# Attention scores copied out of PSUM by ScalarE, and products of a constant at the kernel's start

## The chip, the core and the metric

The kernel runs on one core of a Trainium2 chip. Five engines work side by side, each in the order of its own instructions, and wait for each other by semaphores: TensorE (PE in the profile; its weight loads are listed as PEld), VectorE (DVE), ScalarE (ACT), GpSimd (POOL) and SyncE (SP, which here issues DMAs). Matmul results land in PSUM, eight banks of 2 KB in each partition; TensorE, VectorE and ScalarE work on them there, or on SBUF. The metric is the device time of one execution in microseconds, as the median of several runs. One more execution was profiled; its rows are what the sections below quote.

## The reference

One block of a hybrid decoder, 528 positions (16 learned tokens and 512 real ones) of width 2048. An input projection feeds a state-space mixer and an attention of 16 heads with 64 channels each; both are normalised and go through one output projection, and a gated MLP with a short convolution follows. The part that the change touches is the attention:

```python
z = jnp.einsum('bqhd,bkhd->bhqk', q_blk, k).astype(jnp.float32) * scale
valid = (kpos[None, :] < qpos[:, None])[None, None]
log_keep = jnp.where(valid, jax.nn.log_sigmoid(-z), 0.0)
suffix = lax.cumsum(log_keep, axis=3, reverse=True) - log_keep
w = jnp.where(valid, jnp.exp(jax.nn.log_sigmoid(z) + suffix), 0.0)
return jnp.einsum('bhqk,bkhd->bqhd', w.astype(v.dtype), v)
```

There is no softmax: a reversed running sum over the keys of log(1 + exp(z)) is subtracted from the score, and Exp of that is the weight.

## The kernel before

**Dense work and lanes.** Nearly all of the time is dense products: weights come as tiles of 128 x 1024 floats, are split into a high part (a cast on ScalarE, line 242, tile wh) and a low part (a subtraction on VectorE through the helper of line 117, tile wl), and each product is three matmuls (lines 320 to 322). The attention is no stage of its own. It is a Python generator, `att_lane`, that is stepped between dense products: `pulse` adds up the time of the products issued, and every 900 ns of it one step of the lane is written into the program. So the order of each engine's instructions is fixed when the kernel is built, and dense products stand between the pieces of attention.

**Units and items.** A unit is four heads, and there are four units, 0 to 3. `Unit.items` lists what is done for one: item (0, all four heads), two items of two heads for the second chunk of queries, four items of one head for the third and four for the fourth, and the item None for the last 16 queries. An item goes through four steps, each later by the steps in LAGS (2, 4, 6), while the next items start every two steps:

- `stage_a`: TensorE puts the mask into a bank with a product of a mask and an identity (line 958), then adds the scores (line 969). ScalarE computes Abs of them out of PSUM, then Exp and Ln in SBUF (tile at).
- `stage_a2`: VectorE adds max(z, 0), runs the scan (lines 996 and 999) and subtracts the sum from z (through line 117). Both the first and the last of these read z in PSUM.
- `stage_b`: TensorE transposes the result into a further bank (line 1026; line 1016 for item None), and ScalarE takes its Exp out of that bank.
- `stage_c`: TensorE multiplies with the values (line 1065), VectorE copies the result out (line 1072).

**Banks.** The pool psz has four banks (tag z). An item of the first two chunks takes two of them for its scores; of the third and fourth chunk every second item takes two, one of which (`self.second`) serves the item after it. The transposes take one. A bank is given to a new tile when the readers of the old one are done.

**Other work there.** During units 0 and 1 the dense products are the rest of the input projection, during units 2 and 3 the output projection; then GpSimd adds squares for the next norm (`acc_square`).

**The start.** SyncE issues the loads of x, of the vector tile vec and of the first weights. ScalarE needs x and vec for the first operand. GpSimd fills constants; steady, a tile of ones, is the first operand of the scans.

Of the kernel before, what the change touches and what calls it, by code (L numbers as in the profile page):

```python
# [15 lines left out]
AF = mybir.ActivationFunctionType  # L16
# [44 lines left out]
def build(tc, io, nslots=67, manual=True):  # L61
    nc = tc.nc
    ctx = ExitStack()
    with ctx:
# [51 lines left out]
        def sub(e, out, a, b):  # L116
            e.tensor_tensor(out, a, b, op=ALU.subtract)  # L117
# [16 lines left out]
        def make_consts():  # L134
            G.memset(steady, 1.0)
            S.copy(identb, ident)
# [729 lines left out]
        class Unit:  # L866


            def __init__(self, u):
                self.u = u  # L870
                self.ks, self.qs, self.vts = [], [], []
                self.st, self.yps = {}, {}

# [54 lines left out]
            def stage_a(self, it):  # L928

                if it is None:  # L930
                    n, m = 64, L
                    z = slot([P, L])[:64]
                    for x in range(2):
# [10 lines left out]
                        else:  # L944
                            S.copy(z[:, 264:512], b[:, :248])
                            add(V, z[:, 512:], b[:, 248:], mask5)
                    z = [z]
                else:
# [4 lines left out]
                    if hs[0] % 2 == 0:  # L953
# [8 lines left out]
                        for p in (0, 1) if j == 0 else (hs[0] // 2,):  # L962
                            (kh, kl), (qh, ql) = self.ks[p], self.qs[p]["Q"]
                            for i_, (qq, kk, o) in enumerate(
                                ((self.qf[p], self.kf[p], a),) if j == 0 else ((qh, kh, a - 13), (qh, kl, a - 13), (ql, kh, a - 13))
                            ):
                                for i in range(2):
# [4 lines left out]
                                    )  # L972
                        if j > 1:

                            self.second = zs.pop()
                    else:
                        zs = [self.second]
                    if j == 0:
                        self.kf = self.qf = None
                    z = [b.rearrange("p h k -> p (h k)") for b in zs]  # L980
                t = at_tile(n, m)
                w = m // len(z)
                for x, b in enumerate(z):
                    act(t[:, w * x : w * x + w], b, AF.Abs)
                act(t, t, AF.Exp, scale=-1.0)
# [3 lines left out]
            def stage_a2(self, it):  # L989

                z, t, n, m = self.st[it]
                c = at_tile(n, m)
                w = m // len(z)
                for x, b in enumerate(z):
                    r = slice(w * x, w * x + w)
                    V.scalar_tensor_tensor(t[:, r], b, 0.0, t[:, r], op0=ALU.max, op1=ALU.add)
                w = m if it is None else m // len(it[1])
                for x in range(0, m, w):
                    V.tensor_tensor_scan(
                        c[:, x : x + w][:, ::-1], steady[:n, :w], t[:, x : x + w][:, ::-1], 0.0, op0=ALU.mult, op1=ALU.add  # L1000
                    )
                w = m // len(z)
                for x, b in enumerate(z):
                    r = slice(w * x, w * x + w)
                    sub(V, c[:, r], b, c[:, r])
                self.st[it] = c
# [148 lines left out]
        def square_x(k):  # L1155
# [7 lines left out]
            xraw[k] = None  # L1163

        G.memset(epsc, EPS)
        act(cst.tile([P, 1], F32, name="warm"), epsc, AF.Square)

        load_x(0)
        nc.sync.dma_start(vec, io["vec"])
        fetch(0)  # L1170
        load_x(1)
# [531 lines left out]
```

## Time and profile before

| | us |
|---|---|
| median of 3 runs | 2230.75 (2229.09 to 2231.03) |
| profiled execution | 2228.46 |
| its span, first to last instruction | 2226.7 |
| TensorE busy | 2163.8 (97%) |
| VectorE busy | 1567.0 (70%) |
| ScalarE busy | 1032.5 (46%) |
| GpSimd busy | 209.6 (9%) |
| mean granted clock of TensorE, as a share of full speed | 0.991 |

Times in the rows below are microseconds from the start of the span unless ns is written. Busy time of TensorE is modelled at its ends and includes work at the lower clock, so it says less than it seems to. A row of the timeline gives start, duration, engine, line, operation, what is written and read, a count where equal instructions were merged, and in brackets how long the engine stood idle before it and which instruction ended that. In a table of waits the time is idle time of the waiting engine. A wait for several semaphores is put down to the one that came last.

### The profile page before, as it was taken

Reading aid. Unit: us, or ns where it says so; the run is one execution under the profiler, and the core shown is the slowest. Engines: PE = TensorE matmul, PEld = TensorE weight load, DVE = VectorE, ACT = ScalarE, POOL = GpSimd, SP = SyncE. Lnnn points to the kernel's source line nnn. Section 1 sums busy time; section 2 is a strip of 40 time slices with the busy share of each in tenths; the row PEclk is TensorE's granted clock in tenths of the full one; section 3 lists DMA queues with packets and bytes.
Section 4 is the critical chain, followed back from the end, with each engine's and each line's share of the span. In section 5 each row is a group of like instructions: output and inputs, shape, how many; then the busy total and the mean of one; then the engine's idle time right before and its main releaser. Section 6 shows DMA issues by size and latency. Waiting matters only on the chain.

```text
span 2226.7 us, 39757 instructions
## 1 busy us (share of the span) xinstructions
PE 2163.8 (97%) x16204; PEld 2049.5 (92%) x16204; DVE 1567.0 (70%) x2387; ACT 1032.5 (46%) x1648; POOL 209.6 (9%) x290
## 2 busy tenths in 40 slices
PE   8999999999889999999999999999999999999997
PEld 8999998889778999999999999999999888888887
DVE  7977785765668668788778877887788544444464
ACT  6255444655555455555555555555555222222235
POOL 0000000001112231111101110111010000000004
PEclk9999999999889999999999999999999999999999
DMA  6433333332323357777777777777777533333342
GB/s 220 123 111 101 116 101 120 101 120 96 101 67 119 129 166 180 194 194 207 185 194 200 200 187 193 196 203 188 194 197 206 183 121 118 119 113 120 116 142 76
DMA packets 118806, 335.10 MB, mean 150 GB/s; under 512 B 13024, under 2 KB 25696, under 8 KB 118624
## 3 DMA queue, kind: packets, MB, share of 16 engines
q1 hardware_dynamic: 100288, 269.56, 37.9%
q0 software_dynamic: 17472, 61.89, 13.6%
q8 instruction: 127, 2.08, 0.4%
q10 hardware_dynamic: 864, 1.11, 0.2%
q14 instruction: 55, 0.45, 0.1%
HBM read 300.23 MB, written 32.28 MB: 149 GB/s over the span
## 4 chain that ended last, share of the span: by engine, by line
PE 62%; DVE 2%; ACT 1%; issue 1%; DVEq 0%; ACTq 0%
PE d L321 15%; PE d L320 15%; PE d L322 15%; PE z L321 4%; PE z L320 4%; PE z L322 4%; PE y L321 2%; PE y L322 2%; PE y L320 2%; DVE s L117 0%; DVE wl L117 0%; ACT s L1359 0%; ACT wh L242 0%; ACT s L105 0%; DVE s L114 0%
## 5 line engine op out<-in xcount | busy, mean ns | idle before, releaser
L320 PE MATMUL d<-s,wh 128*128 128x258 f32 (+4 forms) x3456 | 1063.5, 308 | 12.1 <-ACT wh L242 5.6
L321 PE MATMUL d<-s,wh 128*128 128x258 f32 (+4 forms) x3456 | 1057.4, 306 | 1.2 <-DVE s L117 1.2
L322 PE MATMUL d<-s,wl 128*128 128x258 f32 (+4 forms) x3456 | 1052.7, 305 | 1.2 <-DVE wl L117 1.2
L320 PEld LDWEIGHTS d<-s,wh 128*128 128x128 f32 x3456 | 656.4, 190 | 43.8 <-ACT wh L242 7.8
L322 PEld LDWEIGHTS d<-s,wl 128*128 128x128 f32 x3456 | 660.2, 191 | 29.9 <-DVE wl L117 1.8
L321 PEld LDWEIGHTS d<-s,wh 128*128 128x128 f32 x3456 | 658.2, 190 | 30.9 <-DVE s L117 2.5
L242 ACT CAST wh<-wr 128x1024 fp32r<-128x1024 f32 (+2 forms) x209 | 197.4, 945 | 426.6 <-PE d L321 340.9
L117 DVE TENSOR_TENSOR wl<-wr,wh 128x1024 fp32r<-128x1024 f32 (+2 forms) x209 | 232.8, 1114 | 86.5 <-ACT wh L242 86.5
L114 DVE TENSOR_TENSOR s<-s,d 128x512 f32<-128x512 f32 (+2 forms) x176 | 103.6, 589 | 264.1 <-PE d L322 258.9
L321 PE MATMUL z<-s,wh 128*128 128x258 f32 (+1 forms) x768 | 219.5, 286 | 0.0
L320 PE MATMUL z<-s,wh 128*128 128x258 f32 (+1 forms) x768 | 218.7, 285 | 0.5 <-ACT s L1434 0.5
L322 PE MATMUL z<-s,wl 128*128 128x258 f32 (+1 forms) x768 | 217.7, 283 | 0.5 <-DVE wl L117 0.5
L117 DVE TENSOR_TENSOR wl<-wu,wh 128x1024 fp32r<-128x1024 f32 x132 | 161.4, 1223 | 2.8 <-ACT wh L242 2.7
L114 POOL TENSOR_TENSOR s<-s,s 128x514 f32<-128x514 f32 (+1 forms) x73 | 85.0, 1165 | 799.8 <-ACT s L105 669.7
L320 PE MATMUL y<-s,wh 128*128 128x258 f32 (+1 forms) x544 | 155.7, 286 | 0.0
L322 PE MATMUL y<-s,wl 128*128 128x258 f32 (+1 forms) x544 | 154.4, 284 | 1.2 <-DVE wl L117 1.2
L321 PE MATMUL y<-s,wh 128*128 128x258 f32 (+1 forms) x544 | 154.5, 284 | 0.0
L242 ACT CAST wh<-wu 128x1024 fp32r<-128x1024 f32 x132 | 138.8, 1052 | 32.6 <-ACT s L105 32.6
L322 PEld LDWEIGHTS z<-s,wl 128*128 128x128 f32 x768 | 146.6, 191 | 0.7 <-DVE wl L117 0.7
L321 PEld LDWEIGHTS z<-s,wh 128*128 128x128 f32 x768 | 146.9, 191 | 0.0
L320 PEld LDWEIGHTS z<-s,wh 128*128 128x128 f32 x768 | 145.1, 189 | 0.7 <-ACT s L1434 0.7
L117 DVE TENSOR_TENSOR wl<-wu_s,wh 128x1024 fp32r<-128x1024 f32 x88 | 107.5, 1222 | 41.8 <-ACT wh L242 41.8
(224 smaller groups left out, 2769.2 us busy)
## 6 DMA issues: line engine op xcount, KB each, us to landing
wu<-w_up SPq DMA_DIRECT2D x132, 512.0 KB, 5.3
wu_s<-w_up SPq DMA_DIRECT2D x88, 512.0 KB, 4.8
wu_s<-w_up POOLq DMA_DIRECT2D x88, 512.0 KB, 7.4
wr<-w_down SPq DMA_DIRECT2D x96, 384.0 KB, 3.0
wr<-w_in SPq DMA_DIRECT2D x63, 512.0 KB, 4.2
wr<-w_out SPq DMA_DIRECT2D x32, 512.0 KB, 3.9
fact<-s POOLq DMA_DIRECT2D x44, 256.0 KB, 3.1
s<-fact SPq DMA_DIRECT2D x44, 256.0 KB, 3.4
```

The source lines that it names most:

```text
L114: e.tensor_tensor(out, a, b, op=ALU.add)
L117: e.tensor_tensor(out, a, b, op=ALU.subtract)
L242: S.copy(hi[:, r], raw[:, r])
L320: PE.matmul(ps, whi, xhi, start=start, stop=False, **kw)
L321: PE.matmul(ps, whi, xlo, start=False, stop=False, **kw)
L322: PE.matmul(ps, wlo, xhi, start=False, stop=stop, **kw)
```

## The change

**In attention.** `stage_a` takes a slot in SBUF for each item (for two items where one pair of banks serves two), and ScalarE copies the banks there as soon as its turn comes. Abs, the addition of max(z, 0) and the last subtraction read that copy, each with one instruction for an item. The bank of the second item of a pair is copied together with the first one's, and the copy waits in the list `self.zs`.

**At the start.** The memset of steady moves from `make_consts` to the very beginning, ahead of that of epsc. The load of vec is issued by ScalarE ahead of its table load and no longer by SyncE between x and the weights. Nine FP32 products of steady with itself, 264 columns each, into a bank that nobody reads, stand first on TensorE.

```diff
         def make_consts():
-            G.memset(steady, 1.0)
             S.copy(identb, ident)
...
-                        if j > 1:
-
-                            self.second = zs.pop()
-                    else:
-                        zs = [self.second]
+
+                        z = None
+                        for x, b in enumerate(zs):
+                            if z is None or j > 1:
+                                z = slot([P, 528])[:n, :m]
+                                self.zs.append(z)
+                            S.copy(z[:, nh * k * x : nh * k * (x + 1)] if j < 2 else z, b.rearrange("p h k -> p (h k)"))
+                    z = self.zs.pop(0)
...
-                    z = [b.rearrange("p h k -> p (h k)") for b in zs]
                 t = at_tile(n, m)
-                w = m // len(z)
-                for x, b in enumerate(z):
-                    act(t[:, w * x : w * x + w], b, AF.Abs)
+                act(t, z, AF.Abs)
...
-                w = m // len(z)
-                for x, b in enumerate(z):
-                    r = slice(w * x, w * x + w)
-                    V.scalar_tensor_tensor(t[:, r], b, 0.0, t[:, r], op0=ALU.max, op1=ALU.add)
+                V.scalar_tensor_tensor(t, z, 0.0, t, op0=ALU.max, op1=ALU.add)
...
-                w = m // len(z)
-                for x, b in enumerate(z):
-                    r = slice(w * x, w * x + w)
-                    sub(V, c[:, r], b, c[:, r])
+                sub(V, c, z, c)
...
+        G.memset(steady, 1.0)
         G.memset(epsc, EPS)
+
+        nc.scalar.dma_start(vec, io["vec"])
+        load_x(0)
+        fetch(0)
         act(cst.tile([P, 1], F32, name="warm"), epsc, AF.Square)
 
-        load_x(0)
-        nc.sync.dma_start(vec, io["vec"])
-        fetch(0)
+        ps = bank([P, 264])
+        for i in range(9):
+            PE.matmul(ps, steady[:, :P], steady[:, :264], start=True, stop=True)
         load_x(1)
```

The order of TensorE's instructions is otherwise as it was. What changes there is who ends its waits. On TensorE, at the third item of unit 0 (masks into two banks of the pool z, scores, then the transposes of the first item, whose operand is the tile at; the bracket names the engines waited for), there stands before:

```order
L958 LDWEIGHTS identb [waits DVE_49]
L958 MATMUL z_4970<-mask,identb 128x128 [waits PE_49]
L958 LDWEIGHTS identb [waits DVE_49]
L958 MATMUL z_4971<-mask,identb 128x128 [waits PE_49]
...
L1026 MATMUL z_4985<-consts,at_4946 128x116 [waits DVE_49,PE_49]
```

and now:

```order
L956 LDWEIGHTS identb
L956 MATMUL z_4982<-mask,identb 128x128 [waits Activation_49]
L956 LDWEIGHTS identb
L956 MATMUL z_4983<-mask,identb 128x128 [waits Activation_49]
...
L1018 MATMUL z_4999<-consts,at_4960 128x116 [waits DVE_49,Activation_49]
```

The masks waited for VectorE and now wait for ScalarE (Activation); the transposes wait for VectorE and, for their bank, for ScalarE.

On ScalarE, at the first two items of unit 0 (s is a slot in SBUF, at the working tile), before:

```order
L105 ACTIVATE at_4907<-z_4899 116x256 [waits PE_49]
L105 ACTIVATE at_4907<-z_4900 116x256 [waits PE_49]
L101 ACT_TABLE_LOAD
L105 ACTIVATE at_4907<-at_4907 116x512 [waits Activation_49] x2
L105 ACTIVATE at_4941<-z_4931 128x256 [waits PE_49]
L105 ACTIVATE at_4941<-z_4932 128x256 [waits PE_49]
L105 ACTIVATE at_4941<-at_4941 128x512 [waits Activation_49] x2
```

and now:

```order
L977 COPY s_4917<-z_4909 116x256 [waits PE_49]
L977 COPY s_4917<-z_4910 116x256 [waits PE_49]
L105 ACTIVATE at_4920<-s_4917 116x512 [waits Activation_49]
L101 ACT_TABLE_LOAD
L105 ACTIVATE at_4920<-at_4920 116x512 [waits Activation_49] x2
L977 COPY s_4953<-z_4943 128x256 [waits PE_49]
L977 COPY s_4953<-z_4944 128x256 [waits PE_49]
L105 ACTIVATE at_4956<-s_4953 128x512 [waits Activation_49]
L105 ACTIVATE at_4956<-at_4956 128x512 [waits Activation_49] x2
```

Two copies stand ahead of each Abs, which is now one instruction.

## Rows read from the trace of the kernel before

**Rows 1.** The page, part 1: busy us, share of the span, instructions

```profile
PE 2163.8 (97%) x16204; PEld 2049.5 (92%) x16204; DVE 1567.0 (70%) x2387; ACT 1032.5 (46%) x1648; POOL 209.6 (9%) x290
```

**Rows 2.** Table of waits of TensorE: waited for, us in total, times, longest us

```profile
PE z L1026 <- DVE at L117: 25.5, 14, 4.2
PE z L958 <- DVE at L117: 4.7, 6, 1.6
PE z L1016 <- DVE at L117: 2.4, 2, 1.8
```

**Rows 3.** Timeline, unit 0: start us, us, engine, line, operation [idle before, releaser]

```profile
379.39 1.36 DVE L999 TENSOR_TENSOR_SCAN at<-steady,at 116x128 f32<-116x128 f32 x4
380.67 0.73 DVE L117 TENSOR_TENSOR at<-z,at 116x256 f32<-116x256 f32 x2
381.12 0.56 PE L958 MATMUL z<-mask,identb 128*128 128x128 bf16 x2 [0.63 <-DVE at L117]
383.16 0.72 DVE L117 TENSOR_TENSOR at<-z,at 128x256 f32<-128x256 f32 x2
383.70 0.49 PE L1026 MATMUL z<-consts,at 116*128 116x116 f32 x3 [1.46 <-DVE at L117]
...
390.61 0.66 PE L1026 MATMUL z<-consts,at 128*128 128x128 f32 x4 [2.72 <-DVE at L117]
```

**Rows 4.** Timeline, unit 2, where GpSimd adds squares

```profile
561.65 3.48 DVE L999 TENSOR_TENSOR_SCAN at<-steady,at 116x128 f32<-116x128 f32 x4
561.82 2.71 POOL L114 TENSOR_TENSOR s<-s,s 128x514 f32<-128x514 f32 x2 [9.32 <-ACT s L105]
565.50 0.56 PE L958 MATMUL z<-mask,identb 128*128 128x128 bf16 x2 [0.72 <-DVE at L117]
570.81 1.01 PE L1026 MATMUL z<-consts,at 116*128 116x116 f32 x4 [4.19 <-DVE at L117]
```

**Rows 5.** Busy time by stretch at half clock: length, engines (count), PEclk, DMA share, GB/s

```profile
443.80:447.10 3.30, 3.30 (x18) 3.11 (x16) 1.22 (x1) 1.15 (x2) 0.00 (x0) 0.50 0.00 0
...
652.00:655.30 3.30, 2.85 (x13) 2.85 (x14) 2.71 (x6) 1.63 (x4) 0.00 (x0) 0.50 0.00 0
sum 33.30, PE 30.04 PEld 28.64 DVE 15.37 ACT 9.10 POOL 2.40; mean PE 3.76 PEld 3.58 DVE 1.92 ACT 1.14 POOL 0.30
```

**Rows 6.** ScalarE's groups by shape, 350 to 860 us: count, busy us, mean ns, idle

```profile
L915 ACT COPY s<-z 128x512 f32<-128x512 f32 x8 | 4.7, 583 | 5.9 <-PE z L914 5.9
L1309 ACT COPY s<-d 128x256 f32<-128x256 f32 x2 | 0.7, 358 | 0.0
```

**Rows 7.** Busy time by stretch, as in rows 5: unit 0; units 2 and 3

```profile
374.30:433.70 59.40, 52.80 (x491) 46.79 (x490) 41.86 (x77) 37.70 (x74) 0.00 (x0) 1.00 0.25 82
...
552.00:693.50 141.50, 120.46 (x1047) 108.22 (x1045) 98.76 (x171) 78.87 (x155) 21.48 (x24) 0.90 0.28 93
```

**Rows 8.** VectorE's groups by shape, units 2 and 3, columns as in rows 6

```profile
L117 DVE TENSOR_TENSOR at<-z,at 128x512 f32<-128x512 f32 x8 | 5.5, 691 | 0.3
L117 DVE TENSOR_TENSOR at<-z,at 116x256 f32<-116x256 f32 x4 | 1.4, 399 | 0.0
L117 DVE TENSOR_TENSOR at<-s,at 64x528 f32<-64x528 f32 x2 | 1.4, 700 | 0.1
```

**Rows 9.** Timeline of the start, and two pairs of FP32 products at full clock

```profile
0.77 0.54 POOL L135 MEMSET steady<- 128x528 f32 x1
4.19 0.73 ACT L415 ACTIVATE s<-s,vec 128x528 fp32r<-128x528 f32 x1 [1.96 <-DMA vec<-vec]
5.64 0.59 PE L320 MATMUL d<-s,wh 128*128 128x264 f32 x1 [5.64 <-ACT wh L242]
...
10.33 0.29 PE L322 MATMUL d<-s,wl 128*128 128x264 f32 x1
...
41.04 0.61 PE L368 MATMUL y<-s,consts 128*128 128x264 f32 x2
41.49 0.61 PE L368 MATMUL z<-s,consts 128*128 128x264 f32 x2
```

More of the change, by code (lines that the diff above doesn't have):

```diff
@@ L871, in __init__ @@
                 self.ks, self.qs, self.vts = [], [], []
-                self.st, self.yps = {}, {}
+                self.st, self.yps, self.zs = {}, {}, []
             def load(self, what):
@@ L946, in stage_a @@
                             add(V, z[:, 512:], b[:, 248:], mask5)
-                    z = [z]
                 else:
```

## The prediction

> **What bounds the kernel now.** I read the page first, then the table of waits of TensorE, then stretches of the timeline, and last the groups by shape. TensorE is busy for 97% of the span and the chain that ended last is almost all TensorE [rows 1]; the reader should conclude that the only time to win is where TensorE stands idle or runs at its lower clock. The table of waits says where it stands: 25.5 us ahead of the transposes of L1026, 4.7 us ahead of the mask products of L958 and 2.4 us ahead of L1016, 32.6 us together, all put down to the subtraction of stage_a2 on VectorE [rows 2]. That is all in attention, between 374 and 693 us.
>
> The timeline of unit 0 tells what is waited for. The third item's mask product starts at 381.12, in the middle of the first item's pair of subtractions (380.67 to 381.40): it reads nothing that they write, it wants a bank of which they are the last readers. The transposes of the first item start at 383.70, though their operand was complete at 381.40; what ended just then is the first half of the *second* item's pair (383.16 to 383.88). The transposes of the second item start at 390.61 after 2.72 us [rows 3]. So at these places TensorE waits for a bank of the pool z, four banks of which two items hold two each from their scores to their subtraction. Unit 0 loses 0.63 + 0.10 + 1.46 + 2.72 = 4.9 us so, and unit 1 repeats it. Units 2 and 3 lose about 7.7 each, since there GpSimd adds squares at the same time: four scans that took 1.36 us in unit 0 take 3.48 us in unit 2 under a GpSimd addition of 2.71 us, and the transposes then wait 4.19 us [rows 3, 4]. Together some 25 of the 32.6 us are bank waits, and the other 7.5 us lie later in the units, where VectorE is busy without a break and its result itself is late.
>
> The waits cost a second time. After them the granted clock falls to 0.50: in eight stretches of 33.30 us TensorE was busy for 30.04 us at half clock [rows 5], half of which, 15.0 us, is loss. By place, from the eight rows of that view of which the first and the last stand there: 3.0 us follow unit 1's waits, 4.7 us unit 2's, 4.1 us unit 3's, and 3.3 us belong to two later waits of unit 2.
>
> **The change part by part.** *Copies.* 56 copies are added (14 in a unit: 2 of 116x256, 4 of 128x256, 4 of 128x384, 4 of 128x512). ScalarE copies 128x256 out of PSUM in 358 ns and 128x512 in 583 ns [rows 6]; 384 columns lie between, taken as 470. Sum: 24 x 0.36 + 16 x 0.47 + 16 x 0.58 = 25.5 us, 6.4 us in a unit. Abs now reads SBUF, once for an item instead of once for a bank: three fewer in a unit, longer ones, in all about 0.2 us less. ScalarE is busy 37.7 of unit 0's 59.4 us, VectorE 41.9 [rows 7]; ScalarE goes to 44. VectorE's two passes over z do not get faster: the subtraction takes 691 ns for 512 columns out of PSUM and 700 ns for 528 out of SBUF [rows 8], but three pairs become single ones, 0.8 us a unit.
>
> *What the banks' earlier release buys.* A bank now comes free when ScalarE has copied it, not when VectorE has subtracted. I replayed the first items of each unit by hand with the durations above, in the order of each engine. Unit 0: two copies (overlapped, 0.66 us) put Exp and Ln of the first item 0.65 us later, so VectorE ends its subtraction at about 382.1 instead of 381.4. The third item's scores no longer wait. The first transposes wait for their operand alone, about 1.0 us. The second item's operand is ready at 384.8, ahead of its transposes at 386.4, where it took until 390.6. Then a bill comes: the values' product of the second item waits about 0.7 us for its Exp, behind the copies of the fourth item, and the third item's transposes wait about 1.3 us, because VectorE is then continuously at work. So 3.0 us of new waits stand against 4.9. Unit 1 is alike. Unit 2: waits of 1.1 (the slow scans stay), 1.2 (Exp behind three chains), then 1.9 more than now is hidden at the fourth and fifth item, 4.2 in all against 7.7. Unit 3: 1.9 + 0.1 + 0.7 = 2.7. Old 25, new 12.9: **12.2 us** saved. Bounds: all 32.6 us go; or every wait comes back as an operand wait, 0.
>
> *Clock.* The new waits are of about 1 us with work between them, where the old ones were 1.5 to 4.2 us with little between. Unit 0 kept the full clock through 0.63, 1.46 and 2.72 us of waits. I take the three falls behind the first waits as gone, 3.0 + 4.7 + 4.1 = **11.8 us**, and the 3.3 us of the later waits as staying. Bounds: 0 and 15.0.
>
> *What ScalarE's load takes back.* In the later items (384 and 512 columns) two copies, about 0.9 us, stand ahead of Abs on ScalarE for every second item; queued behind them are the Exp for the values' product and the cast of the next weights. Those casts lead by a whole weight tile, so they cost nothing unless ScalarE falls behind by several us. The Exp does not lead so far. I take 1 us a unit, **4 us**; bounds 0 and 12.
>
> *What GpSimd takes back.* The two passes of VectorE that read z will have two SBUF inputs, as the scan has, which a GpSimd addition stretched from 1.36 to 3.48 us [rows 3, 4]. In the 141.5 us of units 2 and 3 GpSimd is busy 21.5 us [rows 7] and the passes over z 28.6 us, in eight groups from 5.5 to 1.4 us [rows 8]: 4.3 us of overlap if they fall together by chance, at a stretch of (3.48 - 1.36) / 2.71 = 0.78 some 3.4 us, half of it on the path, **1.7 us**; bounds 0 and 5. The Trainium skill, "SBUF — State Buffer", Who interferes with whom, speaks against the copy here: a VectorE instruction with two SBUF inputs contends with a GpSimd instruction that reads SBUF, one with at most one does not. By that rule, with which those rows agree (the passes that read z from PSUM keep 691 ns in units 2 and 3, the scan does not keep its time), the copy moves two passes of each item into reach of GpSimd; without it this term would be zero.
>
> *Start.* Nine FP32 products of 264 columns run ahead. Two such start 0.45 us apart at full clock (41.04 and 41.49, [rows 9]), so 0.9 at half. They can start when the memset of steady ends, about 1.3 us. Now TensorE starts at 5.64 and runs at full speed from about 10.3, 4.6 us later [rows 9]. If the clock rises 4.6 us after the first product too, 5.1 products run slow and 3.9 fast, and the real work starts at 7.7 us at full clock: by 10.3 it has done 2.6 us where 4.6 us at half clock did 2.3. That is a gain of 0.3 us. Bounds: all nine slow, work from 9.4, 1.4 us lost; a rise after 2.5 us, work from 6.6, 1.3 us won. I take **0**. vec goes out on ScalarE's queue, ahead of a table load; ScalarE waited 1.96 us for vec there [rows 9], which covers that, and SP's transfers start 0.4 us sooner, which the products cover. The Trainium skill, "TensorE: Matmul & The Clock Gate", Part 1, says that the number of slow matmuls at a kernel's start varies from run to run; no run here shows that yet, and it would make this term differ between two traces of the same kernel.
>
> *Sum.* 12.2 + 11.8 - 4 - 1.7 + 0 = 18.3 us. The profiled execution took 2228.5 us (span 2226.7 and 1.8 around it), so 2210.2; the median of the runs is 2.3 us above it: 2212.5, stated as **2212 us**. What follows attention is bound by TensorE and keeps the gain.
>
> **Rivals.** *ScalarE's chain becomes the bound.* At 44 us of work in a unit that would last some 53, any queueing puts the Exp behind copies. For it: new waits in every replay. Then the waits keep 21 of 25 us and the clock keeps half its falls, less the 4 and 1.7: 4 + 6 - 5.7, some 4 us won, 2226. *All waits go and the clock stays up*: 32.6 + 15.0 = 47.6, so 2183. Against it: VectorE works 42 of 59 us, in long unbroken runs. *Slower: the transposes wait for their operand, not for a bank.* Then only the 4.7 us at L958 go, while copies lengthen the chain from scores to operand by 0.66 us at each of the 12 first items and by about 0.8 us at the ten later waits, 16 us: 11 us lost, 2242. It decides if the operand comes later than the bank at most of the transposes; against it stand 381.40 and 383.70 above. *The copies free nothing sooner*, since ScalarE reaches them late: 2231. Against it: ScalarE mostly waited for the scores (Abs began right after them).
>
> **How the numbers follow.** Forecast (gain of 10 to 30 us) 0.63; ScalarE the bound 0.15; all waits gone 0.07; operand waits 0.08; nothing freed 0.07. A measurement of this kernel tells 0.2% (4.5 us) from no change. Faster: 0.63 + 0.07 + 0.07 of the second = 0.77. Same: the rest of the second and 0.06 of the last, 0.14. Slower: 0.08 + 0.01 = 0.09. The range runs from 2194 (forecast with new waits half as long and no load term) to 2228 (ScalarE the bound, falls kept) and leaves out the two ends, 0.07 and 0.08, and little else.
>
> **What would show it.** After: no wait of the mask products; transposes waiting for the subtraction of their own item, at 1 us or so; waits of the values' product for Exp, which are new; fewer stretches at half clock between 440 and 660 us; copies of 0.36 to 0.6 us; TensorE's first real product near 7.7 us at full clock. I am wrong if the wait at the second transposes (2.72 us in each unit) is still there, if the clock falls as often as before, or if VectorE's passes over z take longer than 0.69 us away from GpSimd.

## The result and the profile after

| | before | after |
|---|---|---|
| median of the runs timed together, us | 2229.92 (2228.9 to 2231.03) | 2203.74 (2201.34 to 2204.2) |
| ratio, with its 95% interval | | 0.988 (0.9863 to 0.9897) |
| span of the profiled execution, us | 2226.7 | 2201.8 |
| mean granted clock | 0.991 | 0.995 |

The change gains 26.2 us by the medians and 24.9 by the two spans. The forecast was 2212 us, a gain of 18: the direction and the range held, and the gain is 8 us larger than its sum.

The page's first part of the changed kernel (busy us, share of the span, instructions), beside [rows 1]:

```profile
PE 2155.4 (98%) x16222; PEld 2042.1 (93%) x16222; DVE 1570.7 (71%) x2363; ACT 1052.7 (48%) x1692; POOL 209.7 (10%) x290
```

ScalarE's busy time rises by 20.2 us and VectorE's by 3.7. The span falls although both work more, so busy time was not what was saved. The table of TensorE's waits of the changed kernel (line waited for: us in total, times, longest us) answers [rows 2]; L956 takes the place of L958, L1018 that of L1026, L1008 that of L1016:

```profile
PE z L1018 <- DVE at L117: 14.3, 15, 2.0
...
PE z L1008 <- DVE at L117: 2.2, 2, 1.7
PE z L1018 <- ACT s L977: 2.1, 1, 2.1
```

The mask products (L956) are gone from the table, and 25.5 us ahead of the second transposes have become 16.4 (14.3 and 2.1). With the 2.2 us ahead of L1008 and a wait of 0.5 us of the values' product for an Exp, 32.6 us of waits have become 19.1.

Unit 0 in the timeline of the changed kernel, first TensorE and then VectorE (start us, us, engine, line, operation, idle before and what ended it), beside [rows 3]:

```profile
380.95 0.29 PE L956 MATMUL z<-mask,identb 128*128 128x128 bf16 x2
...
382.95 0.59 PE L1018 MATMUL z<-consts,at 116*128 116x116 f32 x4 [1.15 <-DVE at L117]
...
387.07 0.66 PE L1018 MATMUL z<-consts,at 128*128 128x128 f32 x4
...
391.03 0.66 PE L1018 MATMUL z<-consts,at 128*128 128x128 f32 x4 [0.82 <-DVE at L117]
...
382.11 0.69 DVE L117 TENSOR_TENSOR at<-s,at 116x512 f32<-116x512 f32 x1
...
390.28 0.69 DVE L117 TENSOR_TENSOR at<-s,at 128x512 f32<-128x512 f32 x1
```

The transposes at 382.95 now follow the subtraction of *their own* item, which ends at 382.80. Those of the second item, which waited 2.72 us before (390.61 in [rows 3]), start at 387.07 without a wait; the ones at 391.03 are the third item's and follow their own subtraction, which ends at 390.97. Before, the transposes of the first and of the second item each waited for the subtraction of a newer item, the last reader of a bank. A wait for the own item's subtraction is the new kind that the forecast named.

The stretches at half clock of the changed kernel (stretch, length, engines, PEclk, DMA share, GB/s) answer [rows 5], where there were eight of 33.30 us:

```profile
492.61:499.44 6.83, 6.66 (x28) 6.34 (x29) 3.63 (x6) 3.63 (x5) 0.00 (x0) 0.50 0.52 190
550.64:554.05 3.41, 3.41 (x20) 2.83 (x19) 0.87 (x3) 1.49 (x5) 0.00 (x0) 0.50 0.60 175
625.73:629.14 3.41, 3.41 (x18) 3.41 (x17) 3.34 (x7) 1.71 (x3) 0.00 (x0) 0.50 0.51 156
sum 13.65, PE 13.48 PEld 12.58 DVE 7.85 ACT 6.83 POOL 0.00; mean PE 4.49 PEld 4.19 DVE 2.62 ACT 2.28 POOL 0.00
```

Half of 13.48 us is lost now, 6.7 us, against 15.0 before: 8.3 us won back. ([rows 5] end each stretch a little early; over the full lengths, 3.41 us and twice that as here, TensorE was busy for 30.7 us at half clock before, and the difference is 8.6 us.)

The copies, by shape, from 350 to 860 us of the changed kernel (count, busy us, mean ns, idle before), beside [rows 6]:

```profile
L977 ACT COPY s<-z 128x512 f32<-128x512 f32 x16 | 8.6, 589 | 9.1 <-PE z L967 9.0
L977 ACT COPY s<-z 128x384 f32<-128x384 f32 x16 | 6.9, 482 | 10.4 <-PE z L967 10.4
L977 ACT COPY s<-z 128x256 f32<-128x256 f32 x16 | 5.1, 368 | 0.0
L977 ACT COPY s<-z 116x256 f32<-116x256 f32 x8 | 2.6, 375 | 8.9 <-PE z L967 8.9
```

They are 56 copies and 23.2 us. The last column points to the reason why they cost so little: ScalarE stood idle for 28.3 us ahead of them, waiting for the scores.

Unit 0, and units 2 and 3 together, by stretch in the changed kernel, beside [rows 7]:

```profile
374.90:431.00 56.10, 52.35 (x491) 46.65 (x490) 41.95 (x71) 42.88 (x85) 0.00 (x0) 1.00 0.26 87
545.00:671.00 126.00, 111.99 (x1046) 100.29 (x1045) 101.31 (x159) 89.24 (x177) 21.55 (x24) 0.97 0.33 104
```

Unit 0 takes 56.1 us in place of 59.4 with the same work on TensorE (491 products), and units 2 and 3 take 126.0 in place of 141.5. ScalarE's 37.7 us in unit 0 became 42.9.

A long scan of VectorE in unit 3 of the changed kernel, and GpSimd's addition at the same time, beside [rows 4]:

```profile
620.78 3.48 DVE L994 TENSOR_TENSOR_SCAN at<-steady,at 116x128 f32<-116x128 f32 x4
...
620.69 2.67 POOL L114 TENSOR_TENSOR s<-s,s 128x514 f32<-128x514 f32 x2 [2.66 <-ACT s L105]
```

The change leaves this stretching of the scans as it was. VectorE's passes over z, now from SBUF, by shape from 545 to 700 us (as [rows 8]):

```profile
L991 DVE SCALAR_TENSOR_TENSOR at<-s,at 128x512 f32<-128x512 f32 x12 | 9.1, 761 | 0.0
L117 DVE TENSOR_TENSOR at<-s,at 128x512 f32<-128x512 f32 x12 | 8.3, 692 | 0.4
```

The subtraction costs 692 ns, as out of PSUM (691). The maximum (L991) does not keep its time: its mean of 761 ns holds one pass of 1.64 us, and there is another of 384 columns. Below stand first a maximum out of PSUM that began while GpSimd was adding, in the kernel before, then that pass of 384 columns in the changed kernel, and the transposes behind it:

```profile
607.22 0.68 DVE L996 SCALAR_TENSOR_TENSOR at<-z,at 128x512 f32<-128x512 f32 x1
606.82 1.31 POOL L114 TENSOR_TENSOR s<-s,s 128x514 f32<-128x514 f32 x1 [9.49 <-DVE s L111]
...
571.69 1.65 DVE L991 SCALAR_TENSOR_TENSOR at<-s,at 128x384 f32<-128x384 f32 x1
571.25 3.23 POOL L114 TENSOR_TENSOR s<-s,s 128x514 f32<-128x514 f32 x2 [12.10 <-DVE s L111]
576.03 0.52 PE L1018 MATMUL z<-consts,at 128*128 128x128 f32 x3 [2.05 <-DVE at L117]
```

From SBUF and away from GpSimd the pass of 384 columns takes 0.55 us and the one of 512 takes 0.68; these two, at 571.69 and 592.75 us, began while a GpSimd addition ran and took 1.65 and 1.64. (One that began just ahead of an addition, at 582.12, kept 0.55.) In the kernel before two maxima began so, at 586.58 and 607.22 us, and kept 0.55 and 0.68 us. This is the price that the forecast had set for the second SBUF input. The additions at 571.25 and 592.52 us are not the squares that the section on the kernel before names: in units 2 and 3 GpSimd also adds x to each finished tile of the output projection (`ssm_done`). What releases such an addition is VectorE's own product (L111), so it starts just as VectorE goes on to its next pass.

At the start (timeline of TensorE, beside [rows 9]) real products begin at 6.80 us, where they began at 5.64, and by 41 us the two kernels stand within 0.12 us of each other:

```profile
1.33 5.82 PE L1167 MATMUL d<-steady 128*128 128x264 f32 x18 [1.33 <-POOL epsc L1158]
6.80 0.48 PE L319 MATMUL d<-s,wh 128*128 128x264 f32 x1
```

### The profile page after: what moved, and what is told of

Its sections match the earlier page's. It is cut to its first block, busy times and chain, and to the rows that moved or that the text cites. A ratio compares the mean times of both kernels' runs of the same rounds, so it can differ in the third digit from the quotient of the medians.

```text
span 2201.8 us, 39840 instructions
## 1 busy us (share of the span) xinstructions
PE 2155.4 (98%) x16222; PEld 2042.1 (93%) x16222; DVE 1570.7 (71%) x2363; ACT 1052.7 (48%) x1692; POOL 209.7 (10%) x290
## 3 DMA queue, kind: packets, MB, share of 16 engines
q0 software_dynamic: 17472, 61.89, 13.7%
## 4 chain that ended last, share of the span: by engine, by line
PE 63%; DVE 2%; issue 1%; ACT 1%; DVEq 0%; ACTq 0%
PE d L320 15%; PE d L319 15%; PE d L321 15%; PE z L320 4%; PE z L319 4%; PE z L321 4%; PE y L320 2%; PE y L319 2%; PE y L321 2%; DVE s L117 0%; DVE wl L117 0%; ACT wh L241 0%; ACT s L1356 0%; DVE s L114 0%; DVE s L111 0%
```

## The experiments

My theory: the gain comes from banks that come free before VectorE has subtracted, so that TensorE waits less and its clock falls less; the new start is worth nothing. Rivals: the start carries some of it; the merged passes or the reads from SBUF carry it; GpSimd's contention takes back a part that could be had; the distance between the steps is what matters, and the bank only by that. The ratios are to runs of the kernel before that were made beside each kernel; the medians of these lie between 2228.72 and 2230.43 us, so a difference of a us or two between two rows says little by itself. "Norm at" is the time in the trace at which TensorE starts the first product of the norm behind attention (826.2 us in the kernel before): it shows what attention alone has won.

| kernel | median, us | ratio (95%) | norm at, us |
|---|---|---|---|
| changed kernel | 2203.74 | 0.988 (0.9863 to 0.9897) | 803.4 |
| new attention, old start | 2204.99 | 0.9891 (0.9877 to 0.9904) | 804.5 |
| old attention, new start | 2228.33 | 0.9995 (0.9986 to 1.0004) | 827.8 |
| copies, bank still held | 2245.55 | 1.0072 (1.0059 to 1.0084) | 841.3 |
| no additions of squares on GpSimd | 2195.76 | 0.985 (0.9836 to 0.9863) | 798.0 |
| passes by halves | 2200.85 | 0.9868 (0.9853 to 0.9883) | 800.9 |
| transposes half a step later | 2198.2 | 0.9856 (0.9841 to 0.9871) | 798.5 |
| transposes a whole step later | 2204.48 | 0.9884 (0.9868 to 0.9901) | 804.1 |
| kernel before, a whole step later | 2215.64 | 0.9934 (0.9919 to 0.9949) | 812.6 |
| half a step later, passes by halves | 2196.27 | 0.9858 (0.9844 to 0.9873) | 794.5 |
| the same, products copied out by ScalarE | 2194.84 | 0.9851 (0.9836 to 0.9866) | 792.5 |
| copies on VectorE | 2220.07 | 0.996 (0.9945 to 0.9975) | 814.8 |
| 6 products at the start | 2202.4 | 0.9885 (0.9868 to 0.9901) | 802.4 |

### The two parts alone

The new attention with the old start. Its edit to the changed kernel takes the start back:

```diff
-        G.memset(steady, 1.0)
         G.memset(epsc, EPS)
-        nc.scalar.dma_start(vec, io["vec"])
+        act(cst.tile([P, 1], F32, name="warm"), epsc, AF.Square)
         load_x(0)
+        nc.sync.dma_start(vec, io["vec"])
         fetch(0)
-        act(cst.tile([P, 1], F32, name="warm"), epsc, AF.Square)
-        ps = bank([P, 264])
-        for i in range(9):
-            PE.matmul(ps, steady[:, :P], steady[:, :264], start=True, stop=True)
```

(`make_consts` sets steady again, as in the kernel before.)

> The new attention (copies by ScalarE, everything else from the copy) with the start of the kernel before. My theory: the whole gain is in the attention units and the new start is worth 0 (between -1.4 and +1.3 us), so the time is that of the changed kernel, 2203 to 2206 us, and the first part up to 41 us stands within 0.3 us of before. Rival: the start carries part of the gain (by an earlier full clock), and the time is 2208 us or more.

Measured 2204.99 us (2204.33 to 2206.72): the attention alone brings 24.6 of the gain by the medians. The expectation for the first part did not hold: at 41 us this kernel stands 0.6 us behind the one before, whose start it has. Its products run at half clock until 12.0 us, those of the kernel before until 10.3.

The other part is the kernel before with the same lines of the start put in.

> The attention of the kernel before with the new start (products of a constant, vec on ScalarE's queue). My theory: no difference from before that can be told, 2229 us to 2231 us; the chain's first product of real operands comes near 6.8 us as in the changed kernel, and what is won there is given back by 41 us. Rival: a gain of 2 us or more that stays.

Measured 2228.33 us (2227.26 to 2232.17), 0.7 us under the range that I gave, ratio 0.9995 with an interval that holds 1. Both runs put the start at some 1.3 us, inside what the comparisons tell from nothing. In the trace the real products begin at 7.07 us and the kernel is 0.7 us ahead of the one before at 41 us; at 862 us it is 1.6 us behind, after clock falls in unit 0 that the kernel before did not have there. The gain is in the attention.

### The copies with the bank held as long as before

```diff
-                w = m // len(z)
-                for x, b in enumerate(z):
-                    act(t[:, w * x : w * x + w], b, AF.Abs)
+                zc = z[0]
+                if it is not None:
+                    zc = slot([P, 528])[:n, :m]
+                    w = m // len(z)
+                    for x, b in enumerate(z):
+                        S.copy(zc[:, w * x : w * x + w], b)
+                act(t, zc, AF.Abs)
```

> The kernel before plus the same copies into SBUF by ScalarE, and Abs reads the copy, but VectorE's two passes (the maximum and the subtraction) still read the PSUM bank, so that a bank is given back as late as before. My theory (what pays is the bank that comes free early): the 25 us of waits of the second transposes for banks stay or grow, and the time is 2229 us to 2242 us. Rival (the saving is in fewer and cheaper passes of ScalarE and in reads from SBUF): 2205 to 2220 us. Second rival (the copies are free load): exactly before, 2229 to 2231 us.

Measured 2245.55 us (2243.59 to 2247.29): 15.9 us slower than before, 42 us slower than the changed kernel, with the same copies (only the second bank of a pair is copied at its own item's turn). Its waits of TensorE:

```profile
PE z L1030 <- DVE at L117: 24.9, 12, 4.0
PE z L958 <- DVE at L117: 10.4, 7, 2.3
```

and the place in unit 0 that [rows 3] showed, TensorE and then VectorE:

```profile
382.76 0.56 PE L958 MATMUL z<-mask,identb 128*128 128x128 bf16 x2 [1.28 <-DVE at L117]
...
382.30 0.73 DVE L117 TENSOR_TENSOR at<-z,at 116x256 f32<-116x256 f32 x2
```

The mask product starts in the middle of the pair of subtractions, as before: it waits until VectorE has read the bank. The 24.9 us ahead of the transposes stay, those of the mask products double, and TensorE is busy at half clock for the time below, in eleven stretches, against 30.04 us in [rows 5]:

```profile
sum 54.60, PE 45.62 PEld 43.23 DVE 28.23 ACT 26.00 POOL 4.86; mean PE 4.15 PEld 3.93 DVE 2.57 ACT 2.36 POOL 0.44
```

Copies and Abs from SBUF bring nothing in themselves; they cost 16 us where VectorE still holds the bank. The size is 3.6 us above the upper end that I gave.

### The passes by halves

```diff
-                act(t, z, AF.Abs)
+                w = m if it is None or it[0] > 1 else m // 2
+                for x in range(0, m, w):
+                    act(t[:, x : x + w], z[:, x : x + w], AF.Abs)
...
-                V.scalar_tensor_tensor(t, z, 0.0, t, op0=ALU.max, op1=ALU.add)
+                h = m if it is None or it[0] > 1 else m // 2
+                for x in range(0, m, h):
+                    r = slice(x, x + h)
+                    V.scalar_tensor_tensor(t[:, r], z[:, r], 0.0, t[:, r], op0=ALU.max, op1=ALU.add)
...
-                sub(V, c, z, c)
+                for x in range(0, m, h):
+                    r = slice(x, x + h)
+                    sub(V, c[:, r], z[:, r], c[:, r])
```

> The changed kernel, but Abs, the maximum and the subtraction of an item that spans two banks run once per half again, as before (from the copies). It takes the fewer and longer passes back and keeps the early release of the banks. My theory (the early release is the gain): by the rows of before one pass of 512 columns is 0.69 us where two of 256 are 0.80, so VectorE has 6 x 0.11 us more in a unit and the whole is 0 to 3 us slower than the changed kernel, 2203 to 2207 us. Rival (merging carries the gain): 2212 us or more.

Measured 2200.85 us (2200.34 to 2201.42): not slower, as I had expected, but 2.9 us faster by the medians, though the two intervals of the ratio overlap. Merging is therefore not what pays. The trace shows why halves help a little: the first transposes of unit 0 (TensorE, then VectorE)

```profile
382.18 0.66 PE L1025 MATMUL z<-consts,at 116*128 116x116 f32 x4 [0.64 <-ACT at L105]
...
381.63 0.74 DVE L117 TENSOR_TENSOR at<-s,at 116x256 f32<-116x256 f32 x2
```

start at 382.18, before the pair of subtractions ends at 382.37 (the bracket names ScalarE, since a pass of it ended last; the first half of the subtraction was done at about 382.0). With one pass over the item they started only when all of it was subtracted, at 382.95. A merged pass saves 0.11 us of VectorE and holds back its first reader for longer than that.

### GpSimd's additions of squares left out

```diff
                 q = slot([P, 528])
                 act(q[:, :n], x, AF.Square)
-                add(G, acc[:, :n], acc[:, :n], q[:, :n])
```

> The changed kernel without GpSimd's additions of the squares (the sums behind the norms are left incomplete, so only times are read). Theory of contention: in units 2 and 3 the scan of 4 x 116 columns that took 3.48 us beside such an addition falls to the 1.36 us it takes in units 0 and 1, PE's waits in unit 2 (5.9 us by the changed kernel's trace) fall to 2 us or less, and the whole is 4 to 7 us faster than the changed kernel (2197 to 2200 us). Rival: the scans are long for another reason (data, their place) and keep 3.48 us; the time stays within 2 us of 2204.

Measured 2195.76 us (2194.99 to 2198.12), 8 us faster than the changed kernel. The scan in unit 3 that took 3.48 us:

```profile
617.65 1.37 DVE L993 TENSOR_TENSOR_SCAN at<-steady,at 116x128 f32<-116x128 f32 x4
```

The contention is shown: without the addition beside it, the scan takes 1.37 us, what it takes in unit 0. But the step from there to the time fell. The waits in unit 2 that I wanted at 2 us or less are 9.7 us in all (10.3 in the changed kernel, where the 5.9 of the expectation are the first five); where a transpose no longer waited for the scan, the values' product waited 1.8 us for its Exp instead. One reason is that this kernel leaves out the squares alone. Of 21.6 us of GpSimd's work in units 2 and 3 some 16 are left, the additions of x, and the maximum that was stretched in the changed kernel is stretched here too:

```profile
567.04 1.66 DVE L990 SCALAR_TENSOR_TENSOR at<-s,at 128x384 f32<-128x384 f32 x1
```

At 548 us, the start of unit 2, this kernel was already 4.2 us ahead: 0.7 us at 447 us, 2.6 more by 500 us, where the clock fall near 492 us did not come, and 0.9 by a wait that it does not have. At 634 us, behind the first parts of units 2 and 3, it was 4.0 us ahead, with falls of its own at 561 and 605 us. So leaving the squares out won nothing in these units on balance; what all of GpSimd's additions cost there no run shows. Of the rest, 1.4 us came by 803 us and 2.0 in the stage behind attention, of which more below.

### The distance of the transposes, with the copies and without

`LAGS` holds how many half steps after the scores VectorE's part, the second transposes and the values' product are issued; an item is two half steps. (The expectations count one unit of `LAGS` as one step.)

```diff
-LAGS = (2, 4, 6)
+LAGS = (2, 5, 7)
```

> The changed kernel with the second transposes one step later behind the subtraction that they read, and the values' product one step later too. My theory: the 18 us of waits left in attention are waits of a transpose for its own item's subtraction, so half of them or more go; 3 to 8 us faster than the changed kernel, 2196 to 2201 us. Rival: ScalarE's or VectorE's throughput holds the units, the waits move to other lines (the values' product for Exp, the next scores) and the time stays within 2 us of 2204.

Measured 2198.2 us (2196.76 to 2199.85), 5.5 us faster than the changed kernel. The intervals of the two ratios overlap a little, but no run of one reaches the other's, and by the trace the norm starts 4.9 us sooner. Its waits:

```profile
PE y L1057 <- DVE s L1064: 5.9, 3, 3.5
PE z L1018 <- DVE at L117: 3.3, 2, 1.8
PE y L1057 <- ACT s L105: 2.8, 1, 2.8
```

The 14.3 us ahead of the transposes are 3.3. A part comes back at the values' product, which now waits for VectorE to copy an older product out of the one bank of pool y.

With (2, 6, 8), a whole step later:

> The changed kernel with the second transposes and the values' product two steps later. My theory: nearly all 18 us of waits go, and with them the falls of the clock inside the units (4 to 7 us); 2192 to 2199 us. Rival: as for one step later, within 2 us of 2204; or the longer-held exponents and copies use up the SBUF slots, and the wait comes back at the copies: 2206 us or more.

Measured 2204.48 us (2204.28 to 2205.09): the rival held, no gain. The transposes' waits are gone from the table, and this took their place:

```profile
PE y L1057 <- ACT s L105: 12.7, 16, 1.5
```

Its ScalarE in unit 0, at the first Exp of a transposed item (128x464), beside the same place one half step earlier in the kernel with (2, 5, 7):

```profile
385.25 0.86 ACT L977 COPY s<-z 128x384 f32<-128x384 f32 x2
386.00 0.54 ACT L105 ACTIVATE at<-s 128x384 f32<-128x384 f32 x1
386.56 1.08 ACT L105 ACTIVATE at<-at 128x384 f32<-128x384 f32 x2
387.55 0.54 ACT L105 ACTIVATE s<-z 128x464 f32<-128x464 f32 x1
```

```profile
385.64 0.55 ACT L105 ACTIVATE s<-z 128x464 f32<-128x464 f32 x1
386.09 0.84 ACT L977 COPY s<-z 128x384 f32<-128x384 f32 x2
```

A whole step later the Exp stands behind the copies and the chain of a newer item, 2.3 us of ScalarE's work; half a step later it stands ahead of them. Of the 2.3 us the two copies are 0.86. The kernel before, at the same distance and without copies, waits 1.9 us there (its table stands below), which points to the copies for most of the 12.7. This is the cost that the forecast feared of them, and it shows only in this order.

The same distance in the kernel before, without copies:

> The kernel before with the second transposes and the values' product two steps later, no copies. My theory: there the transposes wait for a PSUM bank that newer scores hold until their subtraction, and banks go round in the same order whatever the distance of the transposes, so the 25 us of bank waits stay: 2226 to 2234 us. Rival: the distance was the matter in the kernel before too, and it gains as the copies do: 2215 us or less.

Measured 2215.64 us (2213.46 to 2217.56), 14.8 us faster than the kernel before. My expectation failed, and the rival nearly held. The bank waits do not stay:

```profile
PE z L1026 <- DVE at L117: 10.4, 7, 3.6
PE z L958 <- DVE at L117: 8.4, 4, 4.8
...
PE y L1065 <- ACT s L105: 1.9, 4, 0.9
```

I had argued that the banks go round in the same order whatever the distance. What that left out, as I read it now, is that a later claim gives the older holder more time at the places that lost most: 25.5 us became 10.4, and the mask products pay 3.7 of it back. The copies are one of two ways to take these waits away; more than half of their 26 us could be had without them.

### The two that helped, together, and what was left

Half a step later and passes by halves in one kernel:

> The changed kernel with both edits that helped apart: passes by halves, and the second transposes and the values' product one step later. They take the same waits (a transpose for its own item's subtraction), so I expect less than the sum of the two gains of 2.9 and 5.5 us: 2195 to 2199 us. Rival (they are separate): 2195 us or less.

Measured 2196.27 us (2195.64 to 2197.95), inside the range. It is 0.9 us less than the sum of the gains, which does not tell the two theories apart; by the start of the norm the two gain 8.9 us together, and 2.5 and 4.9 alone. The longest waits left were those for the copy out of pool y, so that copy went to ScalarE:

```diff
-                        V.tensor_copy(y[p][:, a + e - T0 : a - T0 + n], yp[:, p, e:])
+                        S.copy(y[p][:, a + e - T0 : a - T0 + n], yp[:, p, e:])
```

> The one before with the copies of the values' products out of PSUM on ScalarE in place of VectorE. With the later transposes the longest waits left were those of the values' product for that copy (3 waits, 5.9 us), which stood behind other passes on VectorE. Theory: they go, 1 to 4 us faster than the one before. Rival: ScalarE's queue (copies, Abs, Exp, Ln) holds it as long: within 1.5 us of it.

Measured 2194.84 us (2193.38 to 2196.53). Those waits are gone from its table; in their place the transposes' waits went from 2.4 to 5.2 us, so 1.4 us by the medians, not to be told from nothing. This is the fastest complete kernel of the study: 8.9 us faster than the changed kernel, and the norm behind attention starts 10.9 us sooner.

### The copies on VectorE

```diff
-                            S.copy(z[:, nh * k * x : nh * k * (x + 1)] if j < 2 else z, b.rearrange("p h k -> p (h k)"))
+                            V.tensor_copy(z[:, nh * k * x : nh * k * (x + 1)] if j < 2 else z, b.rearrange("p h k -> p (h k)"))
```

> The changed kernel with the same copies on VectorE in place of ScalarE. My theory: the copies cost little on ScalarE because it has room there (42.9 us busy of the 56.1 of unit 0, as VectorE has 42.0), but on VectorE they stand in the queue behind passes and scans of up to 3.5 us, so the scores' banks come free later and ScalarE's chain waits for them: 2212 to 2235 us. Rival (either engine has the room, 6.4 us a unit): within 4 us of 2204.

Measured 2220.07 us (2216.23 to 2220.51), 16.3 us slower than the changed kernel. The table of ScalarE's waits has a line that the changed kernel does not have:

```profile
ACT at L105 <- DVE s L977: 63.9, 25, 5.0
```

Abs waits up to 5 us for a copy that stands in VectorE's queue behind passes and scans, and TensorE then waits 21.9 us ahead of the transposes. By their share in unit 0 of the changed kernel the two engines are alike (42.0 and 42.9 us busy), so the share does not tell which of them has room for the copies; what is queued ahead of them does.

### Fewer products at the start

```diff
-        for i in range(9):
+        for i in range(6):
```

> The changed kernel with 6 products of the constant in place of 9 at the start. By its trace the operands of the first real product lay ready at 5.6 us and the constant's products ran until 6.8 us. Theory: real products start at 5.6 to 6 us, partly at the half clock, and by 41 us nothing is left of it, since what comes next there waits for data: within 1 us of 2204. Rival: 1 us or more is kept.

Measured 2202.4 us (2201.19 to 2203.85), 0.6 us below the range that I gave and 1.3 us below the changed kernel, which is not to be told from nothing. Real products start at 6.25 us instead of 6.80. At 41 us this kernel is 0.7 us ahead of the changed one, but the nine traced kernels with nine products differ by 1.0 us there among themselves, so the edit is not shown to have kept anything.

## Why the forecast held, point by point

**What bounds the kernel** was read rightly. TensorE's waits in attention and its half clock behind them are where the gain came from, and 41, 371 and 862 us into the program the changed kernel stands at +0.12, +0.6 and -22.8 us against the one before.

**Banks, 12.2 us.** The mechanism held: no mask product waits, the 2.72 us wait is gone, and the transposes wait for their own item, 1.15 and 0.82 us in unit 0 and up to 2.05 in unit 2. (The wait of 2.1 us in unit 3 that the table puts down to a copy is of the same kind: the subtraction of its item ended at 624.99 us, the copy at 625.06.) By unit the first waits came out as 2.0, 1.5, 5.9 and 2.1 us, 11.4 in all, where 3.0, 3.0, 4.2 and 2.7 were forecast, 12.9. That the sums lie so close is in part luck, since unit 2 was too low and the others too high. That the copies alone do not bring it was shown by holding the bank (2245.55 us).

**ScalarE's load, 4 us.** This was the mis-sized term. The later waits of the units are 7.7 us, as they were before (7.9 by the rows of the table, 7.5 in the prediction), where 5.7 us more had been set for this term and the next. I costed ScalarE by its load and not by whether the copy comes while it is idle, though the prediction had said that it mostly waited for the scores; the rows of the copies show 28.3 us of that idle time for 23.2 us of copies. Here the Exp stays ahead of the newer copies; in the kernel with (2, 6, 8), where it does not, the cost comes, 12.7 us of waits.

**GpSimd, 1.7 us.** This term held, as far as it can be told. Two maxima took 1.65 and 1.64 us in place of 0.55 and 0.68, and the transposes behind each wait 2.05 and 1.84 us; so some 2 us of those waits are the stretching, by my estimate from these rows. The first of them makes up 1.1 us of the 1.7 by which the first waits of unit 2 came out above the forecast. The additions did not fall on those passes by chance, as the prediction took it: VectorE's own product sets them off. For the scan, the return from 3.48 to 1.37 us without the addition agrees with what the Trainium skill, "SBUF — State Buffer", Who interferes with whom, says of a VectorE instruction with two SBUF inputs.

**Clock, 11.8 us.** By place, of the 11.8 us behind the first waits of units 1 to 3 the one fall at 625 us is left, 1.7. The two later falls of unit 2, 3.3 us, which I had as staying, went too. But falls came at 492 and 550 us, 5.0 us, where there had been none, and 8.3 us were won: the size is in part a balance of things that the prediction did not see. Around the fall at 492 us TensorE waits four times for VectorE, 1.2 us together, and 0.4 us for ScalarE; the kernel before has the same four waits there, also 1.2 us, and one of 0.9 for ScalarE, and kept its clock. In the kernel without additions of squares this fall does not come and others come at 561 and 605 us. What decides it, and so a few us of any such change, stays open.

**Start, 0.** It came out as 1.3 us in two comparisons of parts, at the edge of what they can tell. The real work started at 6.80 us, where I had 7.7: the constant's products ran for 5.5 us where I took 6.4, since they ran at full clock from 4.5 us on, 3.2 us after the first of them (one record of them starts every 0.44 us until then and every 0.22 after). But that differs from trace to trace, which the prediction could not show yet: in the nine traced kernels with the same nine products the full clock came between 4.5 and 7.2 us, and real work started between 6.80 and 8.14 us. At 41 us these kernels stand between 40.4 and 41.4 us, and the four with the old start between 41.0 and 41.7.

**The rest.** Added up from 371 to 862 us: 13.7 us less idle time of TensorE and 8.3 us of clock are 22.0 of the 23.4 us by which the two traces move apart there. A further 2.1 us came behind 862 us, in dense work that the change does not touch. So the sum missed in this way: waits fell by 13.5 us where 12.2 - 5.7 = 6.5 were forecast, the clock gave 3.5 us less than forecast, and some 3.5 us came from places that no term had.

The rival that all waits go (2183 us) lies beyond all kernels here; the fastest came 8.9 us nearer to it than the changed kernel. The two slower rivals and ScalarE as the bound did not come about in this kernel. That a copy can come too late to free anything is seen with the copies on VectorE (2220.07), and what copies cost that free nothing with the bank held (2245.55).

## What to carry to other kernels

When a wait names an engine's last pass over a PSUM bank, look whether the waiting instruction reads that pass's result or only wants the bank: the first calls for a shorter chain or a later consumer, the second for a copy by an engine that is idle when the bank fills, or for a later claim on the bank. Cost such a copy by the idle time ahead of it and by what is queued behind it on that engine, not by its busy time alone. After an early release, shift the consumers again by the smallest step that the schedule allows: half a step was worth 5.5 us and a whole step nothing, since it put the next Exp behind a newer item's copies and passes. And when a copy turns an operand in PSUM into a second one in SBUF, look what GpSimd does beside the instruction that reads it: two such passes here took 1.65 and 1.64 us in place of 0.55 and 0.68.

## What was not expected of the hardware

TensorE has the same products in the dense stage behind attention in all these kernels. It waits there four to six times for 0.3 to 1.3 us just behind that norm and then no more; in the kernel before and the changed one it is six times, 4.7 and 4.6 us together, and the clock stays up in both. From the first product of the norm behind attention to the first product of the last, unsplit stage it took 1340.9 us in the kernel before, 1338.7 in the changed kernel and in three near it (old start, halves, 6 products: 1338.71 to 1338.72), 1336.8 without the additions of squares, 1342.3 in the kernel with ScalarE's copies of the products, and 1342.8 with the bank held. The ends of it in the changed kernel's timeline:

```profile
803.41 0.70 PE L367 MATMUL y<-s,consts 128*128 128x258 f32 x2
...
2142.14 0.28 PE L319 MATMUL d<-s,s 128*128 128x256 f32 x1
```

Each kernel was traced once, but four near ones agree to 0.03 us, and so do the kernel before and the one with the new start alone, so this is hardly chance from one execution to the next; from end to end it is 6.0 us, as much as several of the edits above are worth. It is no single event either: between the 1000th and the 7000th product of the stage the kernel before falls behind the changed one evenly, by 1.45 us or 0.24 ns in each product. So it goes with the program, though its code here is the same. Why is open. This is a reason to read the place of an edit from the trace before its worth is read from the total.
